# Macaron FFN decoder layer: the gated products and the down projections' weights at another byte of a 512-byte line, with a pair of weight tiles of their own

## The chip, the core and the metric

The kernel runs on one core of one Trainium2 chip. The metric is the device time of one execution in microseconds. Three runs of the kernel before gave 1134.86, 1134.88 and 1136.32 us (median 1134.88). One further execution was recorded by the hardware profiler.

## What is computed

One decoder layer on 512 tokens of 1024 features, all in float32. The part that the change touches is the two SwiGLU FFNs (`ffn1`, `ffn2`); between them lies a token-mixing layer, behind them a gated embedding and a last norm.

```python
def swiglu(x, w_gate, w_up, w_down):
    return (jax.nn.silu(x @ w_gate) * (x @ w_up)) @ w_down
...
        h = h + 0.5 * swiglu(rmsnorm(h, ffn1_norm[i]), ffn1_w_gate[i], ffn1_w_up[i], ffn1_w_down[i])
...
        h = h + jnp.concatenate([ya, yb], axis=-1) @ w_out[i]
        h = h + 0.5 * swiglu(rmsnorm(h, ffn2_norm[i]), ffn2_w_gate[i], ffn2_w_up[i], ffn2_w_down[i])
        gate = jax.nn.sigmoid(rmsnorm(h, ple_norm[i]) @ ple_w_gate[i] + ple_b_gate[i])
        h = h + gate * (p[i] @ ple_w_proj[i])
```

`D_FF` is 2816, so that a down projection is 2816 by 1024: 22 tiles of 128 rows by 8 tiles of 128 columns.

## The kernel before, in words

**Split weights.** Each float32 operand is used as a rounded part (`whi`, `ghi`, `xfb[..., 0]`) and a rest (`wlo`, `glo`, `xfb[..., 1]`), and each product is three matmuls: hi by hi, hi by lo, lo by hi (L210 to L212, and L526 for gate and up). A weight tile of 128 by 1024 is loaded by SP (L402), cast to `whi` by ACT (L412), and its rest goes to `wlo` by DVE (L413). ACT, DVE, PE and SP keep the order in which the program is written.

**Steps.** An FFN is a list of steps that `run` (L344 on) walks through. Gate and up are done for two tiles of 128 hidden features at a time by a scheme with seven products instead of eight (`Group`): seven steps of 24 matmuls of 256 columns, which read `xfa` and `xfb` as the moving operand. What comes out is gated (L610 to L621) and split into `ghi` and `glo` (L630, L631). Down steps (`down`, L646 on) follow one part later, two among the seven steps of a group: each makes two of the eight output tiles, by 24 matmuls of 512 columns (12 for the first part, which has one group), with `ghi` and `glo` as the moving operand. At the FFN's end the four down steps of the last part stand in a row. A step's weights are split two steps ahead: in the pass in which step i is multiplied, the split of step i+2 is issued behind it, then, for a down step, the sums of step i-1 into `h` (L665). PSUM has three banks named `sm` for down steps; a step uses two.

**Weight tiles.** `whi` and `wlo` have three buffers each in the region that lives through the whole kernel; `whix` and `wlox` are a fourth pair, in the right region of an FFN. In an FFN every fourth split, counted by `turns["whi"]`, takes the fourth pair (L408 on), whatever the step: a buffer is used again four splits later.

**Where tiles begin.** SBUF is cut into a base region, a left and a right one, and the latter two are opened anew for each stage. `PAD` (L58) adds bytes in front of the tiles, and so sets the byte, counted within lines of 512 bytes, at which all of a region's tiles begin (each tile here is a multiple of 512 bytes long). In the built program these are: byte 384 for `raw`, `whi`, `wlo`, `tmp`, `h` of the base; byte 320 for `raw0`, `xfa`, `xfb` of an FFN's left region; byte 384 for `x` in the mixing and embedding stages; byte 384 for everything in a right region: `rawb`, `rawd`, `s1`, `whix`, `wlox`, `g`, `ghi`, `glo`, `ya`, `yb`. A matmul reads 512 bytes per partition of a weight tile and 1024 or 2048 of a moving one, from the tile's byte on.

Of the kernel before, what the change touches and what calls it, by code (L numbers as in the profile page):

```python
# [22 lines left out]
F32 = mybir.dt.float32  # L23
# [4 lines left out]
P = 128  # L28
# [26 lines left out]
)  # L55


PAD = {"sb": 480, "ffn_left": 480, "mix_left": 32, "ple_left": 32, "right": 96}  # L58
HEADS = 16
HD = 64  # L60
GROUPS = 2
# [18 lines left out]
def layer_kernel(ctx: ExitStack, tc: tile.TileContext, a: dict, out: bass.AP):  # L80
# [4 lines left out]
    region = {"left": None, "right": None}  # L85
    names = {}
    count = [0]

    def pad(pool, name):
        count[0] += 1  # L90
        n = PAD[name.replace("1", "").replace("2", "")]
        pool.tile([P, n // 4], F32, tag="pad", name=f"pad_{count[0]}")

    def close_region(side):
        if region[side] is not None:

            if side == "right":
                pad(region[side], side)
            region[side].release()

    def open_region(side, name):
        close_region(side)
        names[side] = name
        region[side] = tc.alloc_tile_pool(name=name, bufs=1, side=side, reuse_waits="tile")
        if side == "left":
            pad(region[side], name)
# [4 lines left out]
    def sb(tag, shape=(P, T), dt=F32):  # L111
        count[0] += 1
        pool = region[REGION[tag]] if tag in REGION else base
        return pool.tile(list(shape), dt, tag=tag, bufs=BUFS.get(tag, 1), name=f"{tag}_{count[0]}")
# [5 lines left out]
        count[0] += 1  # L120
        return psum.tile([P, T], F32, tag=tag, bufs=n, name=f"{tag}_{count[0]}")

    turns = {"mm": 0, "whi": 0, "rawb": 0}

    def mm_ps():

# [3 lines left out]
    def sm_ps():  # L130
        return bank("sm", 3)
# [34 lines left out]
    class Unit:  # L166
# [11 lines left out]
        def split(self, c0, c1):  # L178
            c = slice(c0, c1)
            nc.scalar.copy(self.hi[:, c], self.raw[:, c])  # L180
            nc.vector.tensor_tensor(  # L181
                self.lo[:, c], self.raw[:, c], self.hi[:, c].bitcast(F32), ALU.subtract
            )

    def weights(src, n):
        w = Unit(src, n)
        w.load(0, n)
        w.split(0, n)
        return w.hi, w.lo
# [24 lines left out]
    def accumulate(ps, w, j0, xs, first=True, last=True, tokens=slice(0, T)):  # L214

        whi, wlo = w
        for k, (xhi, xlo) in enumerate(xs):
            c = slice((j0 + k) * P, (j0 + k + 1) * P)
            passes(
                ps, whi[:, c], wlo[:, c], xhi[:, tokens], xlo[:, tokens],  # L220
                first and k == 0, last and k == len(xs) - 1,
            )
# [157 lines left out]
    def also(step, what, fn):  # L380

        if what == "after":
            old = step.after[0] if step.after else lambda: None
            step.after = (lambda: (old(), fn()),) + tuple(step.after[1:])
        else:
            old = getattr(step, what)
            setattr(step, what, lambda: (old(), fn()))

    class Parts:
# [11 lines left out]
            self.raw = sb(tag, (P, 1024))  # L401
            nc.sync.dma_start(self.raw[:, :n], src)  # L402

        def split(self, raw=None):
            raw = self.raw if raw is None else raw
            n = self.n

            x = "x" if names["right"].startswith("ffn") and turns["whi"] % 4 == 3 else ""  # L408
            turns["whi"] += 1
            self.hi = sb("whi" + x, (P, 1024), F32R)  # L410
            self.lo = sb("wlo" + x, (P, 1024), F32R)
            nc.scalar.copy(self.hi[:, :n], raw[:, :n])  # L412
            nc.vector.tensor_tensor(  # L413
                self.lo[:, :n], raw[:, :n], self.hi[:, :n].bitcast(F32), ALU.subtract
            )
            return self.hi, self.lo
# [80 lines left out]
    class Group:  # L497
# [69 lines left out]
        def step(self, i, w, raw, to, fresh, loads, sums, after):  # L567
            parts = {}

            def split():  # L570
                parts[0] = w.split(self.s1 if raw else None)

            def product():
                self.parts = parts[0]
                if i == 1:
                    self.ps["a"] = bank("acc", 2)
                    if self.first:

                        nc.tensor.matmul(
                            self.ps["a"], self.parts[0][:, :P], self.parts[0][:, :T], start=True, stop=True  # L580
                        )
                if to in ("x", "q") and fresh:
                    self.ps[to] = bank("mm", 3)
                self.product(i, to, fresh)

            s = Step(product, loads if callable(loads) else (lambda: self.load(*loads)) if loads else None, sums, split, after, i in (1, 7, 6, 3))
            s.from_right = i == 2 or i in (1, 7) and not self.leads or i == 6 and self.leads
            return s
# [48 lines left out]
    def swiglu(name, xfs, norm, closed, after):  # L637


        shared = {}  # L640
        out_norm = Norm()
        src = a[f"{name}_gu"]
        groups = [Group(src[j], xfs, shared, j) for j in range(sum(G_PARTS))]
        gs = [g.steps() for g in groups]

        def down(part, gs_, i, n, last):  # L646

            nf = 2 * len(gs_)
            w = Parts("rawd")
            ds = D_ORDER[i * n : (i + 1) * n]  # L650
            ps = {}

            def product(gs_=gs_, first=0, end=None):
                end = len(gs_) if end is None else end
                x = [t for g in gs_[first:end] for t in g.out]
                for k, d in enumerate(ds):
                    if first == 0:
                        ps[d] = sm_ps()
                    accumulate(
                        ps[d], (w.hi, w.lo), k * nf + 2 * first, x, first == 0, end == len(gs_)  # L660
                    )

            def add():
                for d in ds:
                    nc.vector.scalar_tensor_tensor(h[d], ps[d], 0.5, h[d], ALU.mult, ALU.add)  # L665
                if last:
                    for d in ds:
                        after(d)

            def add_norm():  # L670
                if last:
                    for d in ds:
                        out_norm.add(h[d])

            step = Step(
                product, lambda: w.load(a[f"{name}_down_{part}"][:, i], n * nf * P), None, w.split,
                (add, add_norm),
            )
            if last and i == 0:
                step.product = lambda: product(end=len(gs_) - 1)  # L680
                step.rest = lambda: product(first=len(gs_) - 1)
            return step


        steps = [gs[j][i] for j, i in ((0, 1), (1, 1), (0, 2), (0, 7), (0, 6), (1, 2), (0, 5), (0, 4), (0, 3))]
        g0, pending = 0, []
        for part, n in enumerate(G_PARTS):
            if part:
                for j in range(g0, g0 + n):

                    here = pending[: -(-len(pending) // (g0 + n - j))]
                    pending = pending[len(here) :]
                    for i in (7, 6, 5, 4, 3) if j == 1 else (1, 7, 6, 4, 5, 2, 3):
                        steps.append(gs[j][i])
                        if i in ((6, 5) if j == 1 else (7, 5)):
                            steps.append(here.pop(0))
            g0 += n
            last = part == len(G_PARTS) - 1
            each = 2
            mine = groups[g0 - n : g0]  # L700
            pending = [down(part, mine, i, each, last) for i in range(ND // each)]
        steps += pending


        norm.behind(steps[2:6], D, lambda r: shared.update(r=r))
        also(gs[-1][3], "after", closed)
        return steps, out_norm
# [5 lines left out]
    def embedding(q):  # L713
# [22 lines left out]
        def out():  # L736
            for i in range(0, 4, 2):
# [3 lines left out]
                nc.gpsimd.dma_start(emb_dram[:, 4 * q + i : 4 * q + i + 2], t)  # L741

        return Step(product, load, None, split, (out,), True)

    h = [sb("h") for _ in range(ND)]
    pad(base, "sb")
    norm = Norm(nc.vector)
    x_ffn1, x_mix = [], []
# [30 lines left out]
    x = x_mix  # L779
# [216 lines left out]
    def finish_group(g, tok):  # L996
        rg = Norm.on_all(tok)
        for j in range(4 * g, 4 * g + 4):
            nc.vector.scalar_tensor_tensor(
                xs[j], xs[j], col("ssm_norm", j), rg, ALU.mult, ALU.mult  # L1000
            )
            yb.append(split(xs[j], "yb"))
# [34 lines left out]
    w = weights(w_in[13], D)  # L1037
    for j in range(ND):
        pz = project(13 + j, w)
        if j < ND - 1:  # L1040
            w = weights(w_in[14 + j], D)
# [15 lines left out]
    for half in range(2):  # L1057
        ps = [mm_ps() for _ in range(NC)]
        for u in range(4):
            whi, wlo = weights(w_v[half, u], 1024)  # L1060
# [9 lines left out]
            for c in range(NC):  # L1070
                for i in range(2):
                    k = 2 * u + i
                    xhi, xlo = (chunk(t, c) for t in x[k])
                    w = slice(i * T, (i + 1) * T)
# [136 lines left out]
    x = x_ple  # L1211
# [90 lines left out]
    for side in region:  # L1302
        close_region(side)
# [90 lines left out]
```

## Time and profile before

| | |
|---|---|
| median of three runs | 1134.88 us |
| the profiled execution's own time | 1135.33 us |
| its span, first to last instruction | 1133.6 us |
| mean granted TensorE clock | 0.994 |
| PE busy (matmuls) | 1093.3 us, 96% |
| DVE busy | 827.7 us, 73% |
| ACT busy | 515.4 us, 45% |
| FFN1, embedding and first loads, about | 0 to 382 us |
| mixing stage, about | 382 to 728 us |
| FFN2, about | 728 to 1074 us |
| gated embedding and last norm, about | 1074 to 1134 us |

Times of the timeline and of windows count from the span's start. In a row of the timeline come the start, the duration, engine and line, the operation, out and in, how many instructions were merged into the row, and the idle time of the engine just before it with what ended it. Matmul durations overlap, so the pace of a run of matmuls is read from their starts. Buffer numbers are left out of names (`raw0` reads as `raw`).

### The profile page before, as it was taken

The page shows a single profiled execution, that of the slowest core. Times are in us where ns is not written, and L with a number is a line of the kernel's source. Part 1 is how long each engine was busy: PE and PEld are TensorE (multiplying, and loading weights), DVE is VectorE, ACT ScalarE, POOL GpSimd, SP SyncE. Part 2 cuts the span into 40 slices and gives each one's busy share as a digit, 9 for nine tenths or more (in the row PEclk, how much of TensorE's full clock was granted, in tenths as well). Part 3 has the DMA queues.
Part 4 walks back from the last instruction along what each step waited for, and adds up shares of the span by engine and source line. Part 5 has one row for each costly group of instructions (what it writes and reads, how often), then busy time and mean ns, then how long its engine had stood idle before and what let it go on. Part 6 is the DMA issues. An engine that isn't in the chain of part 4 may idle for free. (4 is left out here: it accounts for less than half of the span.)

```text
span 1133.6 us, 16731 instructions
## 1 busy us (share of the span) xinstructions
PE 1093.3 (96%) x6778; PEld 974.3 (86%) x6778; DVE 827.7 (73%) x1088; ACT 515.4 (45%) x680; POOL 156.6 (14%) x138
## 2 busy tenths in 40 slices
PE   6899999999999999999999999989999999999997
PEld 4889999999998788777788877888999999999886
DVE  6887777766777687799785554878777677776865
ACT  5654434344344465523553333544434434344555
POOL 1000000000000301476421100000000000000221
PEclk9899999999999999999999999999999999999999
DMA  9566555555622323353322223586565555542512
GB/s 345 141 186 175 163 166 154 136 143 163 186 84 66 90 81 93 95 175 121 122 83 93 79 90 110 146 207 168 167 168 167 158 149 158 142 120 75 167 38 75
DMA packets 46861, 154.34 MB, mean 136 GB/s; under 512 B 5312, under 2 KB 5568, under 8 KB 46784
## 3 DMA queue, kind: packets, MB, share of 16 engines
q1 hardware_dynamic: 34128, 117.98, 31.1%
q0 software_dynamic: 6912, 25.17, 12.5%
q10 hardware_dynamic: 5744, 10.12, 2.7%
q8 instruction: 53, 0.87, 0.3%
q14 instruction: 24, 0.20, 0.1%
HBM read 148.99 MB, written 4.26 MB: 135 GB/s over the span
## 5 line engine op out<-in xcount | busy, mean ns | idle before, releaser
L526 PE MATMUL mm<-xfb,whi 128*128 128x256 f32 x800 | 144.9, 283 | 3.6 <-ACT acc L591 2.5
L526 PEld LDWEIGHTS mm<-xfb,whi 128*128 128x128 f32 x800 | 124.4, 190 | 5.2 <-ACT acc L591 2.7
L526 PE MATMUL mm<-xfb,wlo 128*128 128x256 f32 x400 | 113.0, 283 | 0.1
L413 DVE TENSOR_TENSOR wlo<-raw,whi 128x1024 fp32r<-128x1024 f32 x69 | 84.4, 1223 | 35.9 <-ACT whi L412 35.6
L212 PE MATMUL sm<-ghi,wlo 128*128 128x512 f32 x268 | 105.0, 392 | 1.1 <-DVE wlo L413 1.0
L211 PE MATMUL sm<-glo,whi 128*128 128x512 f32 x268 | 104.5, 390 | 0.2 <-DVE glo L631 0.2
L210 PE MATMUL sm<-ghi,whi 128*128 128x512 f32 x268 | 104.5, 390 | 0.0
L526 PE MATMUL acc<-xfb,whi 128*128 128x256 f32 x528 | 96.4, 284 | 1.4 <-DVE g L610 1.4
L612 ACT ACTIVATE g<-g 128x512 f32<-128x512 f32 x44 | 27.8, 632 | 143.3 <-DVE g L611 143.3
L412 ACT CAST whi<-raw 128x1024 fp32r<-128x1024 f32 x69 | 71.8, 1046 | 40.5 <-DVE raw L536 16.1
L526 PEld LDWEIGHTS acc<-xfb,whi 128*128 128x128 f32 x528 | 82.8, 191 | 2.7 <-issue 1.5
L526 PEld LDWEIGHTS mm<-xfb,wlo 128*128 128x128 f32 x400 | 77.3, 193 | 0.3 <-DVE wlo L413 0.3
L526 PE MATMUL acc<-xfb,wlo 128*128 128x256 f32 x264 | 75.0, 284 | 1.4 <-DVE wlo L413 1.4
L413 DVE TENSOR_TENSOR wlo<-rawd,whi 128x1024 fp32r<-128x1024 f32 (+1 forms) x37 | 41.5, 1121 | 44.4 <-ACT whi L412 44.4
L541 POOL DMA_DIRECT2D raw<-in_ffn_gu x22 | 18.9, 858 | 390.5 <-DMA raw<-in_ffn_gu 157.8
L413 DVE TENSOR_TENSOR wlo<-rawb,whi 128x1024 fp32r<-128x1024 f32 x48 | 58.8, 1224 | 16.6 <-ACT whi L412 16.6
L665 DVE SCALAR_TENSOR_TENSOR h<-sm,h 128x512 f32<-128x512 f32 x96 | 63.3, 684 | 10.2 <-PE sm L212 10.2
L181 DVE TENSOR_TENSOR wlo<-raw,whi 128x1024 fp32r<-128x1024 f32 x44 | 57.9, 1317 | 12.7 <-ACT whi L180 12.5
L253 POOL TENSOR_TENSOR ssum<-ssum,tmp 128x512 f32<-128x512 f32 x27 | 38.2, 1415 | 204.6 <-ACT tmp L252 204.0
L180 ACT CAST whi<-raw 128x1024 fp32r<-128x1024 f32 x44 | 45.7, 1042 | 44.9 <-issue 14.2
L210 PE MATMUL mm<-x,whi 128*128 128x512 f32 x160 | 63.5, 397 | 0.0
L212 PE MATMUL mm<-x,wlo 128*128 128x512 f32 x160 | 62.5, 390 | 0.0
(332 smaller groups left out, 2963.2 us busy)
## 6 DMA issues: line engine op xcount, KB each, us to landing
raw<-in_ffn_gu SPq DMA_DIRECT2D x56, 512.0 KB, 4.5
rawd<-in_ffn_down SPq DMA_DIRECT2D x40, 512.0 KB, 3.7
rawb<-in_ffn_gu SPq DMA_DIRECT2D x32, 512.0 KB, 4.6
raw<-in_w_in SPq DMA_DIRECT2D x29, 512.0 KB, 3.5
s<-in_ffn_gu SPq DMA_DIRECT2D x22, 512.0 KB, 4.8
raw<-in_ffn_gu POOLq DMA_DIRECT2D x22, 512.0 KB, 5.5
s<-in_ffn_gu POOLq DMA_DIRECT2D x22, 512.0 KB, 7.2
raw<-in_w_out SPq DMA_DIRECT2D x16, 512.0 KB, 3.5
```

The source lines that it names most:

```text
L180: nc.scalar.copy(self.hi[:, c], self.raw[:, c])
L181: nc.vector.tensor_tensor(self.lo[:, c], self.raw[:, c], self.hi[:, c].bitcast(F32), ALU.subtract)
L210: nc.tensor.matmul(ps, whi, xhi, start=first, stop=False)
L211: nc.tensor.matmul(ps, whi, xlo, start=False, stop=False)
L212: nc.tensor.matmul(ps, wlo, xhi, start=False, stop=last)
L253: self.engines[i].tensor_tensor(self.totals[i], self.totals[i], sq, ALU.add)
L412: nc.scalar.copy(self.hi[:, :n], raw[:, :n])
L413: nc.vector.tensor_tensor(self.lo[:, :n], raw[:, :n], self.hi[:, :n].bitcast(F32), ALU.subtract)
L526: nc.tensor.matmul(o, wt[:, c], xt, start=fresh and p == m == n == 0, stop=last and n == 2, skip_group_check=True,)
L541: nc.gpsimd.dma_start(w21.raw, self.src[0], accum_op=ALU.add)
L612: nc.scalar.activation(t, t, AF.Silu)
L665: nc.vector.scalar_tensor_tensor(h[d], ps[d], 0.5, h[d], ALU.mult, ALU.add)
```

## The change

The right region of an FFN and that of the embedding stage lose their pad of 96 bytes, and all their tiles begin at byte 480; the right region of the mixing stage keeps it. `whix` and `wlox` no longer stand in a turn with the other three pairs: they take the weights of the down steps, all of them but every second one of the last part (`last and i % 2`). Gate and up, and everything else, turn through the three pairs of the base, which stay at byte 384.

```diff
-PAD = {"sb": 480, "ffn_left": 480, "mix_left": 32, "ple_left": 32, "right": 96}
+
+PAD = {"sb": 480, "ffn_left": 480, "mix_left": 32, "ple_left": 32, "ffn_right": 0, "mix_right": 96, "ple_right": 0}
...
         n = PAD[name.replace("1", "").replace("2", "")]
-        pool.tile([P, n // 4], F32, tag="pad", name=f"pad_{count[0]}")
+        if n:
+            pool.tile([P, n // 4], F32, tag="pad", name=f"pad_{count[0]}")
...
-                pad(region[side], side)
+                pad(region[side], names[side])
...
-    turns = {"mm": 0, "whi": 0, "rawb": 0}
+    turns = {"mm": 0, "rawb": 0}
...
-        def split(self, raw=None):
+        def split(self, raw=None, x=""):
+
             raw = self.raw if raw is None else raw
             n = self.n
-
-            x = "x" if names["right"].startswith("ffn") and turns["whi"] % 4 == 3 else ""
-            turns["whi"] += 1
             self.hi = sb("whi" + x, (P, 1024), F32R)
             self.lo = sb("wlo" + x, (P, 1024), F32R)
...
             step = Step(
-                product, lambda: w.load(a[f"{name}_down_{part}"][:, i], n * nf * P), None, w.split,
-                (add, add_norm),
+                product, lambda: w.load(a[f"{name}_down_{part}"][:, i], n * nf * P), None,
+                lambda: w.split(x="" if last and i % 2 else "x"), (add, add_norm),
             )
```

From L94 to L406 lines of the changed file stand two lower than before (L180 is L182), from L410 on where they stood. Every engine runs the same instructions; PE's, POOL's and SP's order is the same. Three places show what else moved.

The first place is ACT in FFN1's first group, where the down steps of the first part are split: `rawd` is what a down step's weights are loaded into. Before:

```order
L630 CAST ghi_672<-g_609 128x1024 [waits DVE_49]
L412 CAST whi_677<-rawd_512 128x512 [waits DMAHW6_49,PE_49,Activation_49]
L595 COPY p_128_707<-mm_645 128x512 [waits PE_49]
L412 CAST whi_709<-s_92_426 128x1024 [waits DMASW7_49,Activation_49]
L599 COPY u_136_735<-acc_336 128x512 [waits PE_49]
L412 CAST whix_737<-rawd_578 128x512 [waits DMAHW7_49,Activation_49]
L412 CAST whi_767<-raw_423 128x1024 [waits DMAHW4_49,Activation_49]
```

And now:

```order
L630 CAST ghi_672<-g_609 128x1024 [waits DVE_49]
L412 CAST whix_677<-rawd_512 128x512 [waits DMAHW6_49]
L595 COPY p_128_707<-mm_645 128x512 [waits PE_49]
L412 CAST whi_709<-s_92_426 128x1024 [waits DMASW7_49,Activation_49]
L599 COPY u_136_735<-acc_336 128x512 [waits PE_49]
L412 CAST whix_737<-rawd_578 128x512 [waits DMAHW7_49,DVE_49,PE_49]
L412 CAST whi_767<-raw_423 128x1024 [waits DMAHW4_49]
```

Nothing changed places; both `rawd` casts now write the one pair `whix`, two splits apart, and the second has a wait on PE that it did not have: for the product of the first.

The second place is DVE at the end of FFN1, where the last four down steps follow each other; the sums of L665 empty the `sm` banks. Before:

```order
L413 TENSOR_TENSOR wlo_3580<-rawd_3410,whi_3579 128x1024 [waits DMAHW4_49,Activation_49]
L413 TENSOR_TENSOR wlo_3610<-rawd_3445,whi_3609 128x1024 [waits DMAHW5_49,Activation_49]
L665 SCALAR_TENSOR_TENSOR h_98<-sm_3545,h_98 128x512 [waits PE_49]
L665 SCALAR_TENSOR_TENSOR h_102<-sm_3552,h_102 128x512 [waits PE_49]
L203 SCALAR_TENSOR_TENSOR x_3616<-h_98,vec_70,x_3615 128x512 [waits Activation_49]
```

And now:

```order
L413 TENSOR_TENSOR wlox_3580<-rawd_3410,whix_3579 128x1024 [waits DMAHW4_49,PE_49,Activation_49]
L413 TENSOR_TENSOR wlo_3610<-rawd_3445,whi_3609 128x1024 [waits DMAHW5_49,Activation_49]
L665 SCALAR_TENSOR_TENSOR h_98<-sm_3545,h_98 128x512
L665 SCALAR_TENSOR_TENSOR h_102<-sm_3552,h_102 128x512
L794 TENSOR_TENSOR whi_3734<-raw_3733,whi_3734 128x8x16 [waits Activation_49]
```

The third down step's split (the first row) now writes the pair that the first down step is multiplied from, and waits for PE ahead of the sums into `h`; the mixing stage's first weight split (L794) moved up.

The third place is ACT at the change from FFN2 to the embedding stage, where `x` is made out of `h` and the squares `tmp` go to the norm. Before:

```order
L180 CAST whi_10030<-raw_10029 128x1024 [waits PE_49,Activation_49]
L202 ACTIVATE x_9870<-h_104,vec_70 128x512 [waits DVE_49]
L252 ACTIVATE tmp_9874<-h_100 128x512 [waits Pool_49]
L252 ACTIVATE tmp_9877<-h_104 128x512 [waits Pool_49]
L202 ACTIVATE x_9882<-h_101,vec_70 128x512 [waits DVE_49]
L202 ACTIVATE x_9886<-h_105,vec_70 128x512 [waits DVE_49]
L252 ACTIVATE tmp_9890<-h_101 128x512 [waits Pool_49]
```

And now:

```order
L204 ACTIVATE x_9869<-h_104,vec_70 128x512 [waits DVE_49]
L254 ACTIVATE tmp_9873<-h_100 128x512 [waits Pool_49]
L254 ACTIVATE tmp_9876<-h_104 128x512 [waits Pool_49]
L204 ACTIVATE x_9881<-h_101,vec_70 128x512 [waits DVE_49]
L182 CAST whi_10028<-raw_10027 128x1024 [waits PE_49,Activation_49]
L204 ACTIVATE x_9885<-h_105,vec_70 128x512 [waits DVE_49]
L254 ACTIVATE tmp_9889<-h_101 128x512 [waits Pool_49]
```

The cast of the embedding stage's third weight unit moved down, to between the last two `x`, since its buffer is now that of FFN2's last down step.

## The prediction

> **What bounds the kernel now.** I read the page's head and busy times first, then PE's busy time in windows, then the starts of PE's matmuls in the timeline.
>
> ```profile
> span 1133.6 us, 16731 instructions
> ...
> PE 1093.3 (96%) x6778; PEld 974.3 (86%) x6778; DVE 827.7 (73%) x1088; ACT 515.4 (45%) x680; POOL 156.6 (14%) x138
> ```
>
> The windows' columns are: stretch, its length, busy time of PE, PEld, DVE, ACT and POOL, granted clock, DMA share, GB/s.
>
> ```profile
> 240.00:360.00 120.00, 120.00 (x841) 112.40 (x840) 85.97 (x95) 48.53 (x59) 4.28 (x5) 1.00 0.45 126
> 743.80:745.90 2.10, 2.10 (x21) 2.10 (x20) 2.00 (x7) 1.56 (x3) 0.77 (x1) 1.00 0.21 81
> 75.08:92.68 17.60, 17.60 (x137) 16.87 (x135) 14.74 (x19) 6.26 (x8) 0.84 (x1) 1.00 0.68 197
> ```
>
> In the middle of FFN1 PE has no idle time in 120 us, at a granted clock of 1.00. So PE sets the end there, and only two things change the time: how fast matmuls follow each other, and new waits of PE. The change touches both.
>
> **The pace of the matmuls.** Their starts, from PE's timeline:
>
> ```profile
> 365.31 0.39 PE L210 MATMUL sm<-ghi,whi 128*128 128x512 f32 x1
> ...
> 368.03 0.39 PE L210 MATMUL sm<-ghi,whi 128*128 128x512 f32 x1
> ...
> 357.74 0.28 PE L526 MATMUL acc<-xfb,wlo 128*128 128x256 f32 x1
> ...
> 359.15 0.28 PE L526 MATMUL acc<-xfb,wlo 128*128 128x256 f32 x1
> ...
> 743.82 0.28 PE L526 MATMUL acc<-xfb,wlox 128*128 128x256 f32 x1
> ...
> 745.86 0.28 PE L526 MATMUL mm<-xfb,wlo 128*128 128x256 f32 x1
> ...
> 1106.80 0.28 PE L210 MATMUL sm<-x,whi 128*128 128x256 f32 x1
> ...
> 1109.32 0.28 PE L210 MATMUL sm<-x,whi 128*128 128x256 f32 x1
> ...
> 1075.88 0.40 PE L210 MATMUL acc<-x,whi 128*128 128x512 f32 x1
> ...
> 1077.96 0.39 PE L210 MATMUL acc<-x,whi 128*128 128x512 f32 x1
> ```
>
> Down's matmuls have moving operand and weights at byte 384: 12 of 512 columns in 2.72 us, 226.7 ns each. The embedding's 256-column matmuls also read both at 384: 21 in 2.52 us, 120.0 ns. The difference gives 256 columns 106.7 ns and each matmul a fixed part of 13.3 ns. Gate and up read `xfb` at 320 and weights at 384: 12 in 1.41 us, 117.5 ns, a fixed part of 10.8; at their best, 18 in 2.04 us, 113.3 ns, 6.7. The slowest stretch of 512 columns is 9 in 2.08 us, 231.1 ns, 17.8. So the fixed part differs with the place of the operands (10.8 against 13.3), and by something else too (6.7 against 10.8 at the same bytes).
>
> No row has both operands at 480, which is where down's matmuls now stand. I bound the new fixed part by 0 and 17.8 ns. Equal bytes gave 13.3 twice, and the one pair of other bytes 10.8; the new pair is equal again, but elsewhere. I take 10.8, the commonest part in the trace: 2.5 ns less than now.
>
> How many matmuls gain, from the groups by line (the same two counts for L210 and L211):
>
> ```profile
> L212 PE MATMUL sm<-ghi,wlo x268: 389/389/504, 73.0 to 1068.2; 128*128 128x512 f32 x134
> ...
> L212 PE MATMUL sm<-ghi,wlox x84: 388/389/393, 78.7 to 1073.6; 128*128 128x512 f32 x84
> ```
>
> That makes (268 + 84) times 3 = 1056. Of these 96 (two of the last part's steps in each FFN, 24 each) keep weights at 384. Of the first group's, 36 in each FFN lie before a wait for DVE that swallows what they gain (below). That leaves 1056 − 96 − 72 = 888, all where PE is full: 888 × 2.5 ns = 2.2 us less, between 11.8 less (fixed part 0) and 4.0 more (17.8).
>
> The Trainium skill, "TensorE: Matmul & The Clock Gate", section "Back-to-back issue gap", gives an isolated matmul at full clock N/2.4 + 2.5 ns, 215.8 ns for 512 columns. The trace's 226.7 lies above it; if the new place reached that figure, the change would save 888 × 10.9 = 9.7 us of matmul time.
>
> **First group of each FFN: a new wait.** The first part's down steps have 12 matmuls each and stand close together. The first and the second now both use `whix`, so the second's cast waits for the first's product. Rows of ACT, PE and DVE:
>
> ```profile
> 73.46 0.64 ACT L412 CAST whix<-rawd 128x512 fp32r<-128x512 f32 x1
> ```
>
> ```profile
> 75.00 0.40 PE L211 MATMUL sm<-glo,whi 128*128 128x512 f32 x1
> ...
> 93.42 0.50 PE L212 MATMUL sm<-ghi,wlo 128*128 128x512 f32 x1 [0.48 <-DVE wlo L413]
> ...
> 785.62 0.50 PE L212 MATMUL sm<-ghi,wlo 128*128 128x512 f32 x1 [0.54 <-DVE wlo L413]
> ```
>
> ```profile
> 74.27 0.68 DVE L413 TENSOR_TENSOR wlox<-rawd,whix 128x512 fp32r<-128x512 f32 x1
> 75.08 1.23 DVE L413 TENSOR_TENSOR wlo<-raw,whi 128x1024 fp32r<-128x1024 f32 x1
> ...
> 92.68 0.69 DVE L413 TENSOR_TENSOR wlo<-rawd,whi 128x512 fp32r<-128x512 f32 x1
> ...
> 766.47 0.69 DVE L413 TENSOR_TENSOR wlo<-rawd,whi 128x512 fp32r<-128x512 f32 x1
> ```
>
> The first product's last matmul with that weight starts at 75.00 and takes 0.40, so the cast starts at about 75.44 instead of 73.46: 2.0 us later. ACT keeps order, so the next cast goes with it, and DVE's rest at 74.27 and all behind it. From 75.08 to 92.68 DVE works 14.74 of 17.60 us, and its idle 2.86 are waits for ACT's part of its own chain (the gate's activation, `ghi`), which shift with it. So the rest at 92.68 comes 2.0 us late, and PE, which waits for it at 93.42 already, loses the whole 2.0. FFN2 has the same distance: 785.62 − 766.47 = 93.42 − 74.27 = 19.15 us. Twice 2.0: **4.0 us**. The bounds are 0 (if DVE's chain had hidden slack) and 4.0.
>
> **Between: hidden.** In later groups one of the gate casts now comes round after three splits instead of four, and waits for a product:
>
> ```profile
> 139.39 1.98 ACT L412 CAST whi<-raw 128x1024 fp32r<-128x1024 f32 x2
> 145.53 1.05 ACT L630 CAST ghi<-g 128x1024 fp32r<-128x1024 f32 x1 [4.16 <-DVE g L621]
> ```
>
> ```profile
> 144.81 0.69 DVE L621 TENSOR_TENSOR g<-g,acc 128x512 f32<-128x512 f32 x1 [0.20 <-PE acc L526]
> ```
>
> The second of the two casts moves from 140.4 to about 141.9. ACT has 4.16 us of idle behind it, and DVE would be 0.2 late at most, where it waits 0.20 for PE at 144.81 anyway. I take 0. Without that cover each of some 20 groups could lose up to 0.2, 4 us; PE was not waiting for `g` there, so I leave that out. Loads and ACT's and DVE's durations don't depend on the byte (L413 takes 1223 ns from `raw` and 1224 from `rawb` on the page), so nothing for these.
>
> **End of each FFN: a second new wait.** The third of the last four down steps uses `whix` again, two splits behind the first. PE, ACT and DVE:
>
> ```profile
> 364.86 0.39 PE L211 MATMUL sm<-glo,whix 128*128 128x512 f32 x1
> ...
> 1060.24 0.39 PE L210 MATMUL sm<-ghi,whi 128*128 128x512 f32 x1
> ```
>
> ```profile
> 361.81 1.04 ACT L412 CAST whi<-rawd 128x1024 fp32r<-128x1024 f32 x1
> ```
>
> ```profile
> 362.88 1.23 DVE L413 TENSOR_TENSOR wlo<-rawd,whi 128x1024 fp32r<-128x1024 f32 x1 [0.26 <-ACT whi L412]
> ...
> 364.37 1.23 DVE L413 TENSOR_TENSOR wlo<-rawd,whi 128x1024 fp32r<-128x1024 f32 x1 [0.26 <-ACT whi L412]
> 365.51 1.28 DVE L665 SCALAR_TENSOR_TENSOR h<-sm,h 128x512 f32<-128x512 f32 x2
> ...
> 1057.37 1.28 DVE L665 SCALAR_TENSOR_TENSOR h<-sm,h 128x512 f32<-128x512 f32 x2
> ```
>
> The cast waits until 364.86 + 0.39 = 365.25 and starts at 365.30. DVE's rest follows 1.07 later, as now (362.88 − 361.81), at 366.37, the fourth step's at 367.51, and only then, at 368.65, the two sums that empty `sm` banks. The first is done at 369.33; PE needs its bank for the second step's second output, which starts at 368.03 now (quoted above). PE waits 1.3 us. The fourth step's product and the stage behind follow in the same order, so it isn't given back. In FFN2 the sums stand at 1057.37 and PE's output at 1060.24, 0.35 us farther apart than 368.03 from 365.51. But the wait there starts from the first step's product as well, which ends with the start of the second's, 2.72 us ahead of that output in both: 1.3 again. **2.6 us**, between 0 and 2.9 (0.11 more each for PE's restart).
>
> **Embedding.** ACT's third cast now stands between two `x`:
>
> ```profile
> 1074.33 1.34 ACT L202 ACTIVATE x<-h,vec 128x512 fp32r<-128x512 f32 x2 [2.33 <-DVE h L665]
> ```
>
> ```profile
> 1076.33 2.69 POOL L253 TENSOR_TENSOR ssum<-ssum,tmp 128x512 f32<-128x512 f32 x2 [1.49 <-ACT tmp L252]
> ```
>
> ```profile
> 1079.32 0.83 PE L262 MATMUL sm<-ones,ssum 128*128 128x1 f32 x7
> ```
>
> A cast is about 1.0 us (1.04 above), so `tmp` and POOL's sums end at 1080.0 instead of 1079.0, and PE, there at 1079.32, waits **0.7 us** more (between 0 and 1.1).
>
> **The sum.** Waits 4.0 + 2.6 + 0.7 = 7.3 us, matmuls −2.2: +5.1. The profiled execution took 1135.33 us (span 1133.6), 0.45 above the median of 1134.88, so 1140.4 for it and **1140.0** by the median.
>
> **Rivals.** A measurement of this kernel can tell about 0.2%, 2.3 us, from no change. Waits of 7.3 us need 8.2 ns a matmul to be repaid.
> - *The place does nothing*: only equal or unequal matters, so the fixed part stays 13.3 and the waits stay, 1142.2. For it: 226.7 and 120.0 give one fixed part at two sizes. Against it: that is one byte, never 480. The Trainium skill, "SBUF — State Buffer", section "Who interferes with whom", gives PE two independent read ports, for the moving operand and for weights, and nothing about bytes; by it no pair of bytes should matter. The traced 117.5 against 120.0 speaks against it.
> - *Half the fixed part goes*, 6.7 as at 743.82: 888 × 6.6 = 5.9 us less, net +1.4, **1136.3**, no difference that can be told.
> - *Nearly all of it goes*, the other side: a fixed part of 0 to 2.5 saves 9.6 to 11.8 us, net −2.3 to −4.5, 1130.4 to 1132.6. The place is every down matmul where PE is full; it decides from 8.2 ns saved, and is told from 10.8 on. The first group's wait would also be this side's helper if DVE's chain gave way: without its 4.0 us, 6.3 ns would do for 0.2%. For it: down's pace is PE's alone for most of both FFNs. Against it: no stretch in this trace goes under 6.7.
> - *A worse place*, 17.8: 4.0 more, 1146.2.
>
> **Chances.** Forecast and the place that does nothing (fixed part 8 to 15): 0.30 and 0.21, both slower. Half of it: 0.17, of which 0.15 within 0.2%. Nearly all, or half with the waits smaller: 0.25, faster. Worse: 0.07. So faster 0.25, same 0.15, slower 0.60. The likeliest's own range is 1137.5 to 1142.5; the one for 8 in 10 takes in the faster side to its end at 1130.4, and above it the place that does nothing with 2 us for the bounds of the waits not counted: 1130.4 to 1144.2.
>
> **What would show it.** Right or wrong, step by step: starts of `sm<-ghi,whix` in the middle of FFN1, 224 ns apart by the forecast, 226.7 if the place does nothing, under 219 if nearly all goes. PE's wait for `wlo` near 93.4 and 785.6 at 2.5 us instead of 0.5. PE's wait for the sums (L665) between the second step's outputs, 1.3 us in both FFNs. L264 0.7 us late. A window in the middle of FFN1 with PE idle would make the hidden part wrong; PE's other paces are to stay at 117.5 and 120.0.

## The result, and the profile after

The changed kernel takes 1137.08 us (median of 12 runs, 1134.41 to 1139.14); the kernel before took 1135.22 us in its 12 (1134.86 to 1137.24). The ratio of the two is 1.0008, with a 95% interval of 0.9998 to 1.0018: no difference that can be told, where 1140.0 was forecast and 0.60 was put on slower. Five of the 12 runs lie between 1134.41 and 1135.27 us and seven between 1136.92 and 1139.14. The profiled execution took 1135.05 us, 0.28 less than the one of before; it is one of the lower five, so what its trace shows need not hold in full for the upper seven.

The head of its page stands for that equality, and already shows that something else is not equal, since PE is busy 8 us less than before (1093.3):

```profile
span 1133.3 us, 16707 instructions
...
PE 1085.3 (96%) x6778; PEld 960.7 (85%) x6778; DVE 824.6 (73%) x1088; ACT 516.2 (46%) x680; POOL 156.8 (14%) x138
```

So about as much was gained as was lost. Three things happened: the matmuls of gate and up got faster, the new waits came, and a load came late.

**Where it was gained.** PE's timeline in the middle of FFN1, one down step of 24 matmuls and part of the gate step behind it:

```profile
240.83 0.39 PE L212 MATMUL sm<-ghi,whix 128*128 128x512 f32 x1
...
242.91 0.39 PE L212 MATMUL sm<-ghi,whix 128*128 128x512 f32 x1
...
246.32 0.39 PE L526 MATMUL acc<-xfb,whi 128*128 128x256 f32 x2
246.54 0.28 PE L526 MATMUL acc<-xfb,wlo 128*128 128x256 f32 x1
...
248.92 0.28 PE L526 MATMUL acc<-xfb,wlo 128*128 128x256 f32 x1
```

The down matmuls, whose operands were moved, take 5.49 us / 24 = 228.8 ns: 2 ns *more* than before. Within the step, the first nine are 231.1 ns apart (2.08 us, to 242.91) and the other 15 227.3 (3.41 us), close to the old 226.7. The gate and up matmuls, whose operands stand where they stood, take 2.38 us / 21 = 113.3 ns, where before they took 117.5 in the prediction's rows and 117.8 on average. There are seven steps of those to two down steps, so the kernel gains in the middle. The same two matmuls, before:

```profile
99.89 0.28 PE L526 MATMUL mm<-xfb,wlo 128*128 128x256 f32 x1
...
359.27 0.39 PE L210 MATMUL sm<-ghi,whix 128*128 128x512 f32 x1
```

and after:

```profile
100.97 0.28 PE L526 MATMUL mm<-xfb,wlo 128*128 128x256 f32 x1
...
355.55 0.39 PE L212 MATMUL sm<-ghi,whix 128*128 128x512 f32 x1
```

The changed kernel is 1.08 us behind at the first and 3.72 ahead at the second: 4.8 us gained in FFN1 between its first group and its end.

**Where it was lost.** The waits of PE, from its timeline at the places of the prediction and at the start of FFN2:

```profile
92.67 0.50 PE L212 MATMUL sm<-ghi,whix 128*128 128x512 f32 x1 [1.37 <-ACT whix L412]
94.02 0.50 PE L214 MATMUL sm<-ghi,wlox 128*128 128x512 f32 x1 [0.61 <-DVE wlox L413]
...
366.06 0.50 PE L212 MATMUL sm<-ghi,whi 128*128 128x512 f32 x1 [1.15 <-DVE h L665]
...
733.73 0.51 PE L526 MATMUL mm<-xfb,whi 128*128 128x256 f32 x2 [0.87 <-ACT acc L591]
...
786.01 0.50 PE L212 MATMUL sm<-ghi,whix 128*128 128x512 f32 x1 [1.36 <-ACT whix L412]
...
1059.39 0.49 PE L212 MATMUL sm<-ghi,whi 128*128 128x512 f32 x1 [1.15 <-DVE h L665]
```

Before, none of the four for `whix` and `h` was there, and the waits for `wlo` were 0.48 and 0.54. ACT's rows name the cause, a cast that waits for the product of the pair's last use:

```profile
74.15 0.62 ACT L412 CAST whix<-rawd 128x512 fp32r<-128x512 f32 x1 [1.84 <-PE sm L213]
...
361.97 1.05 ACT L412 CAST whix<-rawd 128x1024 fp32r<-128x1024 f32 x1 [3.42 <-PE sm L213]
```

The wait at 733.73 was not foreseen. It begins with a load, as an experiment below shows ("The late load"): SP's queue before, and then after.

```profile
712.22 13.56 SPq L402 DMA_DIRECT2D rawb<-in_ffn_gu  x2
```

```profile
722.02 2.82 SPq L404 DMA_DIRECT2D rawb<-in_ffn_gu  x2
```

FFN2's first `rawb` is asked for 9.8 us later. The orders of the two programs on SP say why (row before, row now):

```
L402 DMA rawb_6454<-in_ffn_gu 128x1024
L404 DMA rawb_6453<-in_ffn_gu 128x1024 [waits PE_49]
```

Before, FFN2's right region and the mixing stage's right region both began at byte 384, and this tile ended where the mixing stage's first `ya` tile begins (163712). Moved by 96 bytes, it ends at 163808, over the first 96 bytes of that `ya`, and so it waits until PE has read `ya`.

### The profile page after: what moved, and what is told of

The parts are those of the page before. It is cut to its first block, busy times and chain, and to the rows that moved or that the text cites. A ratio compares the mean times of both kernels' runs of the same rounds, so it can differ in the third digit from the quotient of the medians.

```text
span 1133.3 us, 16707 instructions
## 1 busy us (share of the span) xinstructions
PE 1085.3 (96%) x6778; PEld 960.7 (85%) x6778; DVE 824.6 (73%) x1088; ACT 516.2 (46%) x680; POOL 156.8 (14%) x138
## 5 line engine op out<-in xcount | busy, mean ns | idle before, releaser
L526 PE MATMUL mm<-xfb,whi 128*128 128x256 f32 x1056 | 183.7, 277 | 4.7 <-DVE g L610 2.3
L413 DVE TENSOR_TENSOR wlo<-raw,whi 128x1024 fp32r<-128x1024 f32 x86 | 105.2, 1223 | 40.6 <-ACT whi L412 40.6
L214 PE MATMUL sm<-ghi,wlox 128*128 128x512 f32 x320 | 127.6, 399 | 2.4 <-DVE wlox L413 2.3
L212 PE MATMUL sm<-ghi,whix 128*128 128x512 f32 x320 | 126.3, 395 | 3.6 <-ACT whix L412 2.7
L213 PE MATMUL sm<-glo,whix 128*128 128x512 f32 x320 | 126.7, 396 | 0.5 <-DVE glo L631 0.5
L413 DVE TENSOR_TENSOR wlox<-rawd,whix 128x1024 fp32r<-128x1024 f32 (+1 forms) x44 | 49.5, 1126 | 69.3 <-ACT whix L412 69.3
L413 DVE TENSOR_TENSOR wlo<-rawb,whi 128x1024 fp32r<-128x1024 f32 x64 | 78.3, 1224 | 25.6 <-ACT whi L412 25.6
L412 ACT CAST whi<-rawb 128x1024 fp32r<-128x1024 f32 x64 | 66.7, 1042 | 30.8 <-DVE rawb L536 28.6
L214 PEld LDWEIGHTS sm<-ghi,wlox 128*128 128x128 f32 x320 | 60.7, 190 | 17.4 <-DVE wlox L413 4.8
L212 PEld LDWEIGHTS sm<-ghi,whix 128*128 128x128 f32 x320 | 60.6, 189 | 17.0 <-ACT whix L412 3.1
L213 PEld LDWEIGHTS sm<-glo,whix 128*128 128x128 f32 x320 | 60.6, 189 | 12.9 <-DVE glo L631 1.1
L526 PE MATMUL mm<-xfa,whi 128*128 128x256 f32 x352 | 63.6, 284 | 5.2 <-ACT rawd L740 5.2
L665 DVE SCALAR_TENSOR_TENSOR h<-sm,h 128x512 f32<-128x512 f32 x96 | 63.1, 684 | 7.4 <-PE sm L214 7.4
```

Of the source, the lines that this page charges most:

```text
L212: nc.tensor.matmul(ps, whi, xhi, start=first, stop=False)
L213: nc.tensor.matmul(ps, whi, xlo, start=False, stop=False)
L214: nc.tensor.matmul(ps, wlo, xhi, start=False, stop=last)
L413: nc.vector.tensor_tensor(self.lo[:, :n], raw[:, :n], self.hi[:, :n].bitcast(F32), ALU.subtract)
L526: nc.tensor.matmul(o, wt[:, c], xt, start=fresh and p == m == n == 0, stop=last and n == 2, skip_group_check=True,)
```

## Experiments

In these, "steady pace" is the mean distance of matmul starts from 110 to 350 us and from 805 to 1045 us, where PE is nearly always full; the few distances over 300 ns, at waits of PE, are left out. Lines in edited kernels stand up to 18 lower.

**Only the bytes.** The kernel before with the pads of the change:

```diff
-PAD = {"sb": 480, "ffn_left": 480, "mix_left": 32, "ple_left": 32, "right": 96}
+PAD = {"sb": 480, "ffn_left": 480, "mix_left": 32, "ple_left": 32, "ffn_right": 0, "mix_right": 96, "ple_right": 0}
```

> Only the pads of the change: right FFN tiles at byte 480, the fourth weight pair in its turn with the other three as before. So no new wait, and most down matmuls read their moving operand at 480 and weights at 384. In the changed kernel such down steps (the last part's odd ones) ran at 233 ns a matmul instead of 226.7. Theory A (gate and up's pace is a state that the down step ahead leaves behind, and down at 480/480 leaves the fast one of 113.3 ns): the time depends on what 480/384 leaves. Fast state: about 3200 x 4.4 ns less for gate and up, 5 us more for down, 1126. Slow state of 117.8 ns: 1140. Theory B (gate and up go faster since the tiles that ACT and DVE use no longer begin at PE's byte): 113.3 and 1126. Theory C (gate and up go faster since their weights come from three tiles only): 117.8 and 1140.

Measured 1136.63 us, ratio 1.0014 (1.0005 to 1.0023). PE's timeline, first a gate step from the fourth pair (byte 480), then a down step from a base pair (384) with `ghi` and `glo` at 480, and the gate step behind it:

```profile
208.13 0.28 PE L527 MATMUL mm<-xfb,wlox 128*128 128x256 f32 x1
...
210.65 0.28 PE L527 MATMUL mm<-xfb,wlox 128*128 128x256 f32 x1
...
241.81 0.39 PE L213 MATMUL sm<-ghi,wlo 128*128 128x512 f32 x1
...
246.71 0.39 PE L213 MATMUL sm<-ghi,wlo 128*128 128x512 f32 x1
...
247.17 0.28 PE L527 MATMUL acc<-xfb,wlo 128*128 128x256 f32 x1
...
249.21 0.28 PE L527 MATMUL acc<-xfb,wlo 128*128 128x256 f32 x1
```

That is 21 matmuls in 2.52 us (120.0 ns), 21 in 4.90 (233.3) and 18 in 2.04 (113.3). Gate and up at base pairs go at the quick pace, so the bytes and not the assignment bring it: theory C falls. My 1126 missed by 10.6 us. Every fourth gate step pays 120.0 here, which I had not counted: some 5 us (840 matmuls, 6.6 ns each). FFN2's load came late here too, and by 746 us 2.7 us were gone. The rest isn't traced.

**Only the assignment.** The changed kernel with all pads as before:

```diff
-PAD = {..., "ffn_right": 0, "mix_right": 96, "ple_right": 0}
+PAD = {..., "ffn_right": 96, "mix_right": 96, "ple_right": 96}
```

> Only the assignment of the change: the fourth pair for down steps, all pads as before (everything on the right at 384). All new waits stay. Theories A and B: gate and up stay at 117.8 ns and down at 226.7, so the waits stand bare: 9 us over before by the sum of the steps in the trace of the changed kernel (2.3, 2.1, 2.4, 1.9, 0.3), about 1144. Theory C: gate and up at 113.3, as in the changed kernel, 1137. My prediction's own 7.3 us of waits would give 1142.5.

Measured 1142.93 us against 1135.52, ratio 1.0073 (1.0056 to 1.0090): 7.4 us slower. PE's timeline, gate and up in the middle:

```profile
280.11 0.28 PE L526 MATMUL acc<-xfb,wlo 128*128 128x256 f32 x1
...
283.64 0.28 PE L526 MATMUL mm<-xfb,wlo 128*128 128x256 f32 x1
```

30 matmuls in 3.53 us, 117.7 ns: no gain. So the waits stand bare, and the total is close to the 7.3 of the prediction. Starts of the same matmuls in this trace and that of before give 2.2 and 1.8 us for the two first groups (from before the first down step to where the distance stays the same), 1.5 and 1.6 for the two ends, 0.2 for the embedding.

**Only the operands of down.** The changed kernel, with small gaps between tiles so that in the right region of an FFN only four tags begin at 480:

```diff
+    AT = {'ghi': 480, 'glo': 480, 'whix': 480, 'wlox': 480}
...
+                now = AT.get(tag, 384)
+                gap = (now - last.get(key, now)) % 512
...
+                    pool.tile([P, gap // 4], F32, tag="gap" + tag, name=f"gap_{count[0]}")
```

> The changed kernel, but in the right region only ghi, glo, whix and wlox begin at byte 480; g, rawb, rawd, s1, p7, u2 begin at 384 as before. Same waits. Theory A: as the changed kernel, gate and up at 113.3, 1137. Theory B: gate and up back at 117.8, 1146.

Measured 1134.24 us, ratio 0.9989 (0.9980 to 0.9999), 8.7 us under the run with the assignment alone. PE's timeline, and SP's:

```profile
239.77 0.28 PE L540 MATMUL mm<-xfb,wlo 128*128 128x256 f32 x1
...
242.15 0.28 PE L540 MATMUL mm<-xfb,wlo 128*128 128x256 f32 x1
```

```profile
712.32 13.56 SPq L418 DMA_DIRECT2D rawb<-in_ffn_gu  x2
```

21 in 2.38 us, 113.3 ns, though `g`, `rawb`, `rawd` and `s1` are back at 384. So it isn't what ACT and DVE use: theory B falls. And the load of `rawb` is back at its old time.

**Two kinds of down step in turn.** This asks directly whether gate and up inherit their pace. `ghi` and `glo` at 384; of each two down steps the first reads weights at 480, the second at 384:

```diff
+    AT = {'ffn1_right': {'whix': 480, 'wlox': 480}, 'ffn2_right': {'whix': 480, 'wlox': 480}}
...
-                lambda: w.split(x="" if last and i % 2 else "x"), (add, add_norm),
+                lambda: w.split(x="" if i % 2 or (last and i) else "x"), (add, add_norm),
```

> Tests theory A inside one kernel: ghi and glo at 384 as before; the first down step of each two reads weights from the fourth pair at 480, the second from a base pair at 384; gate and up always from base pairs. Theory A: gate and up steps behind a 384/384 step go at 117.8 ns and those behind a 384/480 step at another pace, likely 113.3, turn by turn, at the same bytes of their own. If instead the pace belongs to the whole kernel or to gate and up's own operands, all steps have one pace.

One run, 1140.38 us. PE's timeline: the gate steps between a 384/384 step (165.33 to 170.78) and the next down step, then those behind a 384/480 step (182.09 to 187.5):

```profile
171.02 0.28 PE L540 MATMUL mm<-xfb,wlo 128*128 128x256 f32 x1
...
181.62 0.28 PE L540 MATMUL mm<-xfb,wlo 128*128 128x256 f32 x1
...
188.64 0.28 PE L540 MATMUL acc<-xfb,wlo 128*128 128x256 f32 x1
...
193.06 0.28 PE L540 MATMUL mm<-xfb,wlo 128*128 128x256 f32 x1
```

90 matmuls in 10.60 us are 117.8 ns; 39 in 4.42 us are 113.3. The same instruction on operands at the same bytes has two paces, and where PE is full the down step ahead of it chooses: from 130 to 350 us and from 830 to 1045 us all 30 down steps are followed by the pace of their kind, turn by turn. There theory A is shown.

Ahead of these stretches PE waits at several places, and there it doesn't always hold. Two of the ten down steps there, each with a wait of PE inside it, are followed by the other pace. The first is this 384/480 step with the gate steps behind it:

```profile
121.01 0.51 PE L228 MATMUL sm<-ghi,wlox 128*128 128x512 f32 x1 [0.72 <-DVE wlox L427]
...
126.50 0.28 PE L540 MATMUL acc<-xfb,wlo 128*128 128x256 f32 x1
...
131.80 0.28 PE L540 MATMUL mm<-xfb,wlo 128*128 128x256 f32 x1
```

45 in 5.30 us are 117.8 ns, the slow pace. And between two down steps, at 114.00 us, the gate steps go from 117.8 to 113.3 behind a wait of 0.20 us, with no down step in between. So a wait of PE can go with a change of the pace too, one way or the other. In the two stretches above PE has none.

**Other places for the moving operand.** The kernel before, with only `ghi` and `glo` moved, to another byte in each FFN (the same gaps, `AT` for `ghi` and `glo` alone). The embedding stage's right region begins at 480 as in the change, which costs nothing that the traces show. One run each; since single runs of before lie up to 4 us apart, the paces count here and not the times.

> The kernel before (fourth pair in its turn, no new waits, all weights at 384), but ghi and glo begin at byte 320 in FFN1 and 352 in FFN2. Looks for a place of the moving operand alone that leaves gate and up at 113.3 ns without the new waits. Theory A (the down step ahead sets the state): unequal bytes leave the fast state, as 480/384 did in the run with the bytes only, so 113.3 in at least one FFN; down at 226 to 233. If the place is not what sets the state: 117.8 in both, 1135.

> The same with ghi and glo at byte 416 in FFN1 and 448 in FFN2. Theory A: 113.3 for gate and up in at least one, down at 226 to 233; against it 117.8 in both and 1135.

> The same with ghi and glo at byte 256 in FFN1 and 128 in FFN2. Theory A: 113.3 for gate and up in at least one, down at 226 to 233; against it 117.8 in both and 1135. Byte 128 lies farthest from 384, so if only the distance matters, FFN2 has the fastest down steps of these three runs.

The steady paces, with those of before and of the runs above (moving operand / weights):

| bytes of the down steps | where | down, ns | gate and up behind, ns |
|---|---|---|---|
| 384 / 384 | before, both FFNs | 226.7 | 117.8 |
| 480 / 480 | changed kernel, both | 228.8 | 113.4 |
| 480 / 384 | only the bytes, both | 233.3 | 113.7 |
| 384 / 480 | two kinds in turn, both | 233.8 | 113.7 to 114.0 |
| 320 / 384 | FFN1 | 233.1 | 113.4 |
| 416 / 384 | FFN1 | 233.2 | 113.4 |
| 256 / 384 | FFN1 | 233.3 | 113.3 |
| 352 / 384 | FFN2 | 233.4 | 117.8 |
| 448 / 384 | FFN2 | 229.6 | 117.7 |
| 128 / 384 | FFN2 | 226.8 | 117.8 |

The times were 1135.15, 1132.42 and 1132.93 us beside 1135.33 for before. The middle one's timeline shows both paces in one run:

```profile
200.35 0.28 PE L541 MATMUL mm<-xfb,wlo 128*128 128x256 f32 x1
...
203.75 0.28 PE L541 MATMUL acc<-xfb,wlo 128*128 128x256 f32 x1
...
906.20 0.28 PE L541 MATMUL acc<-xfb,wlo 128*128 128x256 f32 x1
...
911.15 0.28 PE L541 MATMUL mm<-xfb,wlox 128*128 128x256 f32 x1
```

30 in 3.40 us, 113.3 ns, in FFN1 at 416; 42 in 4.95 us, 117.9 ns, in FFN2 at 448. Each run did what was expected by theory A, but that unequal bytes leave the quick pace isn't the rule: 352, 448 and 128 differ from 384 too and leave the slow one. No byte of these gave both quick paces. That all slow ones lie in FFN2 leaves a doubt, which the next run takes up.

**Byte 416 in both FFNs.**

```diff
+    AT = {'ffn1_right': {'ghi': 416, 'glo': 416}, 'ffn2_right': {'ghi': 416, 'glo': 416}}
```

> The kernel before with only ghi and glo moved, to byte 416 in both FFNs (in e6 FFN1 had 416 and was fast, FFN2 had 448 and was slow). No new wait. If the byte sets the state: gate and up at 113.4 ns in both FFNs, down at 233.3, 3 us less in each FFN's middle, 0.5 us more at each end: 5 us less, 1130.4. If FFN2 is slow for another reason than the byte: 117.8 there and 233 for down, 3 us more there: about 1135.

Measured 1130.18 us, ratio 0.9956 (0.9944 to 0.9968); gate and up at 113.4 in both FFNs, down at 233.2. So 416 is quick in FFN2 as well, as the 1130.4 of the expectation had it. This leaves all weight pairs and their order alone, so no cast waits for a product that it didn't wait for before.

**The new waits taken away.** First by giving the base pairs to more down steps:

```diff
-                lambda: w.split(x="" if last and i % 2 else "x"), (add, add_norm),
+                lambda: w.split(x="" if (last and i) or (part == 0 and i % 2) else "x"), (add, add_norm),
```

> The changed kernel, but the second and fourth down step of the first part and the second to fourth of the last part take a base pair, so that the fourth pair is never used twice within two splits. The waits of the first group, of the end and PE's half clock at 96 us should go. Theory A: gate and up keep 113.3 where a 480/480 step leads, 4.8 and 4.7 us less per FFN stay, 1.3 us more for the mixed down steps: 1126 to 1127. If the waits were not what cost the time (the measured 1137 being a slower pace): 1135 or more.

Measured 1134.72 us, ratio 0.9994 (0.9984 to 1.0003). The stop at the ends went (FFN1's end costs 0.5 us where the changed kernel loses 1.9), but not the loss around the first group. PE's timeline:

```profile
92.94 0.50 PE L212 MATMUL sm<-ghi,whix 128*128 128x512 f32 x1 [0.80 <-ACT whix L412]
...
115.25 0.39 PE L526 MATMUL mm<-xfa,wlo 128*128 128x256 f32 x1 [0.30 <-DVE wlo L413]
...
122.25 0.50 PE L214 MATMUL sm<-ghi,wlox 128*128 128x512 f32 x1 [0.71 <-DVE wlox L413]
```

Everything else now shares three base pairs there, so other splits wait instead; and FFN2's load was late. By the starts of the same matmuls the first groups cost 2.6 and 2.5 us and the load 1.2, most of the 8 us by which I missed. The second try keeps the old turn of four through the first group and gives the fourth pair to down steps from the second part on:

```diff
+            if names["right"].startswith("ffn") and names["right"] not in own:
+                x = "x" if turns["whi"] % 4 == 3 else ""
+                turns["whi"] += 1
...
-                lambda: w.split(x="" if last and i % 2 else "x"), (add, add_norm),
+                lambda: (
+                    w.split(x="" if last and i else "x"), own.add(names["right"]) if part == 0 and i == 3 else None
+                ), (add, add_norm),
```

> The bytes of the change, with the four pairs in their old turn through the first group, the fourth pair for the down steps of parts 1 to 4 and for the last part's first alone. So the new waits of both ends go and the 480/480 down steps of the middle stay. Theory A: gate and up at 113.3 and down at 228.8 in the middle, 4.8 us less in each FFN, 0.5 more at each end (last three down steps at 480/384), up to 1 us lost where FFN2's start waits for a load: 1127 to 1128. If the first group still makes PE wait longer, since DVE and not PE sets its end: 1130.

Measured 1131.43 us, ratio 0.9967 (0.9955 to 0.9979). FFN1 was 5 us quicker than before, but 4.1 of these were gone at FFN2's start, where PE's timeline has three waits:

```profile
730.53 0.51 PE L530 MATMUL mm<-xfb,whi 128*128 128x256 f32 x2 [1.01 <-ACT acc L595]
...
738.19 0.50 PE L530 MATMUL acc<-xfb,whi 128*128 128x256 f32 x2 [0.95 <-ACT whi L416]
739.45 0.58 PE L530 MATMUL acc<-xfb,wlo 128*128 128x256 f32 x1 [0.76 <-DVE wlo L417]
740.26 0.41 PE L530 MATMUL acc<-xfb,wlo 128*128 128x256 f32 x1
740.90 0.41 PE L530 MATMUL acc<-xfb,wlo 128*128 128x256 f32 x1
```

The last two rows are three matmuls apart, 213 ns each: the granted clock is 0.50 from 740 to 742 us, which is part of the loss.

**The late load.** Two kernels put `rawb` back: the last one with only down's operands at 480, and the changed kernel with `rawb` alone at 384.

```diff
+    AT = {'ffn1_right': {'ghi': 480, 'glo': 480, 'whix': 480, 'wlox': 480}, 'ffn2_right': {'ghi': 480, 'glo': 480, 'whix': 480, 'wlox': 480}}
```

> The run with the pairs in their old turn through the first group, but with only ghi, glo, whix and wlox at byte 480; rawb and the rest of the right region back at 384. In that run and in the changed kernel FFN2's first load of rawb was issued some 10 us later than before, since rawb at 480 also lies over the mixing stage's first ya tile, and FFN2's start then lost 4.1 us. If that is the cause, the load is back at its old time and the 4 us come back: 1127.5. If FFN2's start loses them anyway (because it waits for other loads): 1131.4 again.

```diff
+    AT = {'ffn1_right': {'rawb': 384}, 'ffn2_right': {'rawb': 384}}
...
+                now = AT[key].get(tag, 480)
```

> The changed kernel with rawb alone at byte 384, everything else of it as it is: the load of rawb for FFN2 is issued at about 712 us instead of 722. If the late load costs the changed kernel time beside the new waits: 1 to 3 us less than it, 1134 to 1136, and PE's wait at 733.7 gone. If not: 1137.

The first took 1129.16 us, ratio 0.9948 (0.9934 to 0.9962): the lowest ratio of all, though not told from the 0.9956 of byte 416. SP's queue in the kernel without and with this edit:

```profile
718.68 2.82 SPq L405 DMA_DIRECT2D rawb<-in_ffn_gu  x2
```

```profile
707.95 13.56 SPq L419 DMA_DIRECT2D rawb<-in_ffn_gu  x2
```

The load is 10.7 us earlier, and from 696 to 757 us this run loses 0.3 us on the trace of before, where the other had lost 4.1 by 746 us and 3.5 by 757. It still missed 1127.5, by 1.7 us. As much is lost in FFN2 from 800 to 815 us, where PE waits 0.19, 0.20 and 0.71 us and did not before. The second took 1134.47 us, ratio 0.9995 (0.9986 to 1.0004), with the load at 712.23 and no wait at 733. Its interval overlaps that of the changed kernel, so the 1 to 3 us of `rawb` alone are seen in the traces and agree with the medians, but its time by itself doesn't settle them.

## Why the prediction was wrong

- **The new waits: right in place and size, with some luck in the sum.** Forecast 7.3 us, measured 7.4 with the assignment alone. The two ends were put at 1.3 each and showed a wait of 1.15 and a loss of 1.5 to 1.6 (with PE's restart); the first groups at 2.0 each gave 2.2 and 1.8; the embedding gave 0.2 instead of 0.7. Ahead of FFN1's first down step that trace is 1.0 us in front of the one of before, and it loses as much in the mixing stage and at FFN2's start; neither was forecast, and they cancel. In the first group the wait took another form than forecast: not one of 2.5 us for `wlo`, but 1.37 and 0.61, and then matmuls at half the clock (below).
- **The middle is hidden: right.** In the run with the assignment alone the distance to before stays at 1.15 us from 143 to 343 us, to a hundredth: a gate cast that waits for a product there costs nothing.
- **The pace: the step that failed.** "888 × 2.5 ns = 2.2 us less" was counted on the down matmuls, and "PE's other paces are to stay at 117.5 and 120.0". It was the other way round: the down matmuls got 2.0 ns slower, and gate and up 4.4 ns quicker. A group has 168 of the latter and 48 of the former, so it gains 168 × 4.4 − 48 × 2.0 = 0.64 us. Each FFN has eight groups with such full down steps, 5.1 us; 4.8 and 4.6 are seen in the changed kernel's trace. The bytes of the four operand tags gave 8.7 us (1142.93 against 1134.24), not 2.2. The view for it had been quoted: gate and up at 113.3 ns and 117.5 ns with operands at the same bytes (and 512 columns at 226.7 and 231.1, both at 384/384). I made bounds for the down matmuls of these and did not ask what changed between the two places. In the trace of before, FFN1's gate step ahead of the first down step (69.57 to 72.29 us, 24 matmuls) has the quick pace, and the one behind it (75.47 to 78.29) the slow one. But that pair alone would not have shown the cause. In FFN2 the gate step ahead of the first down step is slow, the one behind it is quick (767.92 to 770.30, 21 in 2.38 us), and the slow pace stays from the second down step on.
- **Loads: wrong.** The words "so nothing for these" stood on durations, 1223 and 1224 ns of L413; both were read from tiles at byte 384, so they could not show it. For L413 it was right: with `rawb` at 480 the changed kernel's page has 1224 too. But a region's byte also says which tiles of the stage before lie under a tile, and so what its load waits for. In the changed kernel's trace this cost 1.2 us at FFN2's start, and 4.1 in the kernel that reached it earlier.
- **The place does nothing**, the rival that the Trainium skill ("SBUF — State Buffer", section "Who interferes with whom", two independent read ports for PE) would back, is out: moving four tags by 96 bytes moved the time by 8.7 us. For the down matmuls alone it was nearly right (228.8 against 226.7). **Nearly all of it goes** named about the right gain, 9.6 to 11.8 us, on the wrong matmuls; down's steady pace never went under 226.7. **Half the fixed part goes** has 1136.3, close to the median, and that is luck: no down matmul gained 6.6 ns.
- The sum as measured: 7.4 of waits, −8.7 by the operands, and the late load's 1 to 3, gives −0.3 to +1.7 us, where 0.9 was measured by the ratio and 1.9 by the medians.

What stays open: why 480/480, 384/480, and 480, 416, 320, 256 at weights of 384 leave the quick pace and 384, 352, 448, 128 the slow one, and which pace a wait of PE leaves. Bytes 352, 448 and 128 were tried in FFN2 alone, and 256 and 320 in FFN1 alone. Why the changed kernel's runs spread over 4.7 us where those of before spread over 2.4 wasn't tried either; since a wait of PE can leave either pace, runs might differ there, but only one run has a trace.

## What to carry to other kernels

When the pace of one instruction differs between two places of a trace at the same operands, look at what ran before it, a wait of the engine included, and count every matmul behind a moved one, not the moved ones alone. When a region is shifted, even by 96 bytes, compare which tiles of the earlier stage each of its tiles lies over, and the waits of its first loads. And give a buffer of its own to one kind of step only where that step's turns are far enough apart: a pair used again within two splits cost 7.4 us here, while moving one operand by 32 bytes and leaving the turn alone brought 5.

## What the runs showed of the hardware

- A matmul of 256 columns behind its weight load, operands at 320 and 384, runs at 113.3 or 117.8 ns, where PE is full for all of the 72 or 96 matmuls between two down steps but the first few. Which of the two it is follows from the bytes of the down step ahead as long as PE doesn't wait (30 of 30 steps of the kernel with two kinds in turn); behind a wait of PE either was seen. At 320/480 it takes 120.0. A matmul of 512 columns takes 226.7 to 233.8 on average by the bytes of its operands.
- TensorE's clock fell by half after short waits. Windows of the changed kernel (stretch, length, busy time of PE, PEld, DVE, ACT, POOL, granted clock, DMA share, GB/s):

```profile
92.00:94.00 2.00, 0.73 (x2) 0.30 (x2) 1.87 (x3) 1.10 (x3) 0.00 (x0) 1.00 0.27 102
94.00:96.00 2.00, 1.99 (x7) 1.63 (x8) 1.10 (x1) 0.81 (x1) 0.85 (x1) 0.76 0.50 117
96.00:98.00 2.00, 2.00 (x7) 1.63 (x6) 1.53 (x2) 2.00 (x4) 0.00 (x0) 0.50 0.92 180
```

Waits of 1.37 and 0.61 us, with two matmuls of 512 columns between them, were followed by a clock of 0.50 and down matmuls 427 ns apart. In the kernel with the old turn through the first group, 0.95 and 0.76 us at FFN2's start were followed by 0.50 as well. In the kernel before, 0.48 and 0.69 us left the clock at 1.00. The Trainium skill, "TensorE: Matmul & The Clock Gate", section "What's actually happening", lets the clock fall after one idle window of about 3.4 us; here it fell with 2.0 us of waiting in all (1.7 in the other kernel). In the kernel with the assignment alone the same half clock is there, and the wait for `wlo` at 96.95 is not: I take it that the slower matmuls mostly filled that wait, since the loss of 2.2 us is hardly more than the 2.0 that were forecast for the chain of DVE.
